# Attention of a hybrid decoder trunk: each group's tiles head by head, GpSimd's sums of weights issued after the values, VectorE's beside them, and two small steps of the row maxima on other engines

## The chip, the cores and the metric

The kernel runs on one core of a Trainium2 chip. The metric is the device time of one execution in microseconds (us). The core's engines are TensorE (PE in the profile; PEld is its loading of weights), VectorE (DVE), ScalarE (ACT), GpSimd (POOL) and SyncE (SP, which issues the DMAs). Each engine works through its own queue in order.

## The reference: what is computed

One decoder layer over 4096 positions of width 1024. An RMSNorm, one input projection, three token mixers side by side (a gMLP, a gated linear recurrence, and a forgetting attention), a gate for each, one output projection and a final RMSNorm. The change lies in the attention, 8 heads of 64:

```python
c = jnp.cumsum(jnp.transpose(log_f, (0, 2, 1)), axis=-1)
for blk in range(seq // C_BLOCK):
    ...
    s = jnp.einsum('bhqd,bhkd->bhqk', qh[:, :, q0:q1], kh[:, :, :q1]) * scale
    s = s + c[:, :, q0:q1, None] - c[:, :, None, :q1]
    s = jnp.where(mask[None, None], s, -jnp.inf)
    p = jax.nn.softmax(s, axis=-1)
    outs.append(jnp.einsum('bhqk,bhkd->bhqd', p, vh[:, :, :q1]))
```

## The kernel before

The program has three stages: the projection with the two other mixers (to about 1676 us), the attention (to about 3120 us), and the output projection.

The attention goes over 32 units. A unit is a pair of heads `p` (0 to 3) and a block `Q` of 512 queries (0 to 7). It has `4 * (Q + 1)` blocks of 128 keys; four of them are a group, so a unit has Q + 1 groups and there are 144 groups. The last group of a unit lies on the diagonal: its tiles are 512, 384, 256 and 128 queries wide, and each needs a mask.

For each key block and head one tile (n counts a group's eight tiles, 0 to 7) is made like this: two matmuls write the scores, keys by queries, into PSUM (`st`, lines 1374 and 1377, three buffers); ScalarE takes the exponential into `pt` (line 1381, 13 buffers); on the diagonal GpSimd masks a 128x128 piece of `pt` (line 1386). The tiles of a group are made in the order block 0 head 0, block 0 head 1, block 1 head 0, and so on. The products with the values (`pv`, line 1274, 16 matmuls for a group, two of them side by side in the array) come one group later: between the scores of tiles 2 and 3 of the following group.

The softmax divides by the sum of the weights over the keys. Each head has an SBUF tile `acc` of 128x512 into which the `pt` tiles are added (line 1261, or 1259 for the first two of a unit, 1257 for a copy): VectorE does it for head 0, GpSimd for head 1. A matmul with ones then sums `acc` over partitions (`pl`, line 1223). `finish_unit` follows: ScalarE copies `pv` out (1217) and makes 1/`pl` by Ln and Exp (1227, 1228), VectorE refines it (1230, 1231), GpSimd multiplies (1232, 1233, 1235), and a DMA stores `d_yc` (1236).

The row maxima for the softmax are computed ahead, by products of their own. `rowmax` makes two 128x512 tiles of scores at a time (`sm`, line 127, two buffers of two banks each), and VectorE reduces them from PSUM (line 140, or 135 on the diagonal). A group of the main loop takes four such steps (after tiles 0, 1, 4 and 6); more only while their count lags. When a unit's maxima are there, `rm_tail` makes its row: a maximum over the columns (159), the addition of `cref` (163), the negated copy `m2` (169), its rest in lower precision (170), some steps of the generator later a transposition on TensorE (`mt`, line 1181, which uses one of the two `sm` buffers) and a copy `mr` (1183).

TensorE's order is the order of the code. On the other engines a scheduler sets the order by its own estimate of when things are ready:

```python
ctx.enter_context(tc.manual_schedule(engines={mybir.EngineType.PE}))
```

Of the kernel before, what the change touches and what calls it, by code (L numbers as in the profile page):

```python
# [10 lines left out]
F32 = mybir.dt.float32  # L11
# [4 lines left out]
AF = mybir.ActivationFunctionType  # L16
ALU = mybir.AluOpType
# [4 lines left out]
P = 128  # L22
# [11 lines left out]
def tile_trunk(  # L34
# [16 lines left out]
    nc = tc.nc  # L51
    _, S, D = x.shape
    KC = D // P
    NSB = S // 256
    NJ = S // 512
# [22 lines left out]
    U0 = min(3, 2 * (NB - 1))  # L78
# [77 lines left out]
    def rm_rows(p, Q, mp, mm, m2):  # L156

        if Q > 0:
            nc.vector.tensor_reduce(mm, mp[:, :, : Q + 1], axis=AX.X, op=ALU.max)
            src = mm  # L160
        else:
            src = mp[:, :, 0]
        nc.vector.tensor_tensor(
            mm.rearrange("p (h i) -> p h i", h=2),
            src.rearrange("p (h i) -> p h i", h=2),
            bcast(cref[:, Q, 2 * p : 2 * p + 2][:, :, None], [P, 2, 4]),
            op=ALU.add,
        )
        nc.vector.tensor_scalar(m2[:, 0:8], mm, -1.0, None, op0=ALU.mult)
        nc.vector.scalar_tensor_tensor(  # L170
            m2[:, 8:16], mm, -1.0, m2[:, 0:8].bitcast(F32), op0=ALU.mult, op1=ALU.subtract
        )
# [919 lines left out]
    with ExitStack() as p2:  # L1092
        fs = p2.enter_context(tc.tile_pool(name="fs", bufs=3))
        ac = p2.enter_context(tc.tile_pool(name="ac", bufs=2))
# [18 lines left out]
        units = [(p, Q) for p in range(4) for Q in range(NJ)]  # L1113
        NU = len(units)
# [58 lines left out]
        def rm_tail(u, mp):  # L1173
            p, Q = units[u]
            mm = fs.tile([P, 8], F32, tag="mm", name="mm")
            m2 = fs.tile([P, 16], F32R, tag="m2", name="m2")
            rm_rows(p, Q, mp, mm, m2)
            for _ in range(2 if u == 0 else 3):
                yield
            pt = ps_sm.tile([16, P], F32, tag="sm", name="mt")  # L1180
            nc.tensor.transpose(pt, m2.bitcast(F32), ident)
            mr = fs.tile([16, P], F32R, tag="mr", name="mr", bufs=8)
            nc.vector.tensor_copy(mr, pt)
            mrow[u] = mr

        def unit_load(u):

            load_qa(u)
            qc = qc_t[u % 2]
            mr = d_m[u] if u < U0 else mrow.pop(u).bitcast(F32)  # L1190
            for r in range(2):
                nc.sync.dma_start(
                    qc[66 + r : 67 + r, :, :].rearrange("o h (i c) -> o (h i) c", c=P).bitcast(F32),
                    mr[8 * r : 8 * r + 8, :],
                )
# [42 lines left out]
        def q0_of(u, kb):  # L1238
            p, Q = units[u]
            j = kb - 4 * Q  # L1240
            return max(j, 0) * P, j >= 0

        fin = []

        first_pt = {}

        def do_acc(u, kb, h, pt):

            p, Q = units[u]
            q0, _ = q0_of(u, kb)  # L1250
            if kb == 0:
                if u not in acc_of:
                    acc_of[u] = [ac.tile([P, 512], F32, tag=f"acc{i}", name=f"acc{i}") for i in range(2)]
                first_pt[h] = pt
            eng, a = (nc.vector, nc.gpsimd)[h], acc_of[u][h]
            if Q == 0 and kb == 0:
                eng.tensor_copy(a, pt)
            elif Q and kb == 1:
                eng.tensor_tensor(a, first_pt[h], pt, op=ALU.add)
            elif kb:  # L1260
                eng.tensor_tensor(a[:, q0:], a[:, q0:], pt[:, q0:], op=ALU.add)  # L1261

        def do_pv(u, j, group):

            p, Q = units[u]
            nkb = 4 * (Q + 1)
            if j == 0:
                pv_of[u] = ps_pv.tile([P, 512], F32, tag="pv", name="pv")
            pv = pv_of[u]
            vt = v_t[p * NJ + j]  # L1270
            for kb, pts in group:
                q0, _ = q0_of(u, kb)
                for h in (1, 0):
                    nc.tensor.matmul(  # L1274
                        pv[64 * h : 64 * h + 64, q0:], vt[:, kb % 4, 64 * h : 64 * h + 64], pts[h][:, q0:],
                        start=kb == 0, stop=kb == nkb - 1,
                    )

            for kb, pts in group:
                do_acc(u, kb, 0, pts[0])  # L1280
            if j == Q:
                fin.append(finish_unit(u))
                tick(fin)
            if Q == NJ - 1:
                slots[0] += 2
                vslots[0] += 1
# [5 lines left out]
        def load_wo():  # L1292
            k = len(wo_hi)
            raw = big.tile([P, D], F32, tag="big", name="wor")
            hi = big.tile([P, D], F32R, tag="big", name="woh")
            lo = big.tile([P, D], F32R, tag="big", name="wol")
            nc.sync.dma_start(raw, wv[:, k, :])
            nc.scalar.copy(hi, raw)
            nc.vector.tensor_tensor(lo, raw, hi.bitcast(F32), op=ALU.subtract)
            wo_hi.append(hi)  # L1300
            wo_lo.append(lo)
# [16 lines left out]
        def load_next():  # L1318
            _, kind, i = need.popleft()
            slots[0] -= 1  # L1320
            if kind:
                vslots[0] -= 1
                load_ka(i)
            else:
                load_kb(i)

        def can_load():
            return slots[0] > 0 and (need[0][1] == 0 or vslots[0] > 0)
# [4 lines left out]
        def rm_step():  # L1333
            if not rm_live[0]:
                return

            while need and rm_next_kb() not in kb_t:
                assert can_load()
                load_next()
            try:  # L1340
                next(rm)
                rm_count[0] += 2
            except StopIteration:
                rm_live[0] = False
# [21 lines left out]
        def do_tile(u, kb, h):  # L1366

            p, Q = units[u]
            g = p * NJ + kb // 4
            cs = slice((kb % 4) * P, (kb % 4) * P + P)  # L1370
            q0, diag = q0_of(u, kb)
            qm = min(q0, 256)
            st = ps_st.tile([P, 512], F32, tag="st", name="st")
            nc.tensor.matmul(  # L1374
                st[:, qm:], ka_t[g][:, h, cs], qa_t[u % 2][:, h, qm:], start=True, stop=False
            )
            nc.tensor.matmul(  # L1377
                st[:, qm:], kb_t[g][0:68, h, cs], qc_t[u % 2][:, h, qm:], start=False, stop=True
            )
            pt = pp.tile([P, 512], F32, tag="p", name="pt")  # L1380
            nc.scalar.activation(  # L1381
                pt[:, q0:], st[:, q0:], AF.Exp, bias=bias_of[u][:, h, kb : kb + 1]
            )
            if diag:

                nc.gpsimd.affine_select(  # L1386
                    pt[:, q0 : q0 + P], pt[:, q0 : q0 + P], pattern=[[1, P]], compare_op=ALU.is_ge,
                    fill=0.0, base=0, channel_multiplier=-1,
                )
            return pt  # L1390

        pend, group = None, []
        for si, (u, kb) in enumerate(steps):
            p, Q = units[u]
            nkb = 4 * (Q + 1)
            while p * NJ + kb // 4 not in ka_t:
                load_next()
            if need and can_load() and need[0][0] < si + 48:
                load_next()
            elif not need and not rm_live[0] and len(wo_hi) < KC and slots[0] >= 3 and si % 2:  # L1400
                load_wo()
                slots[0] -= 2
            pts = []
            for h in range(2):
                pts.append(do_tile(u, kb, h))
                n = 2 * (kb % 4) + h
                if h == 1:
                    do_acc(u, kb, 1, pts[1])
                if n in (0, 1, 4, 6):
                    rm_step()  # L1410
                if n in (3, 5, 7) and rm_count[0] < 2 * si + LEAD:
                    rm_step()


                if n == 2 and pend is not None:
                    do_pv(*pend)
                    pend = None
                if n in (4, 5, 7):
                    tick(fin)
            group.append((kb, pts))  # L1420
            if kb % 4 == 3:
                pend, group = (u, kb // 4, group), []
            if kb == max(0, nkb - 4) and u + 1 < NU:
                while u + 1 >= U0 and u + 1 not in mrow:
                    rm_step()
                unit_load(u + 1)
                unit_bias(u + 1)
        do_pv(*pend)
        drain(fin)
        while len(wo_hi) < KC:  # L1430
# [106 lines left out]
```

## Time and profile before

| | before |
|---|---|
| median of 3 runs | 3488.28 us |
| lowest to highest | 3479.05 to 3490.75 us |
| profiled execution | 3480.39 us, span 3478.6 us |
| mean granted TensorE clock | 0.973 |
| PE, DVE, ACT, POOL busy | 96%, 69%, 46%, 42% of the span |
| attention, 1676 to 3120 us | 1444 us of the span |

The span is the time from the first to the last instruction of the profiled execution. A line number such as L1261 is the line of the kernel before. A busy PE is modelled: a half-speed clock shows in the column PEclk and not as idle time, so both have to be read.

### The profile page before, as it was taken

Reading aid. Unit: us, or ns where it says so; the run is one execution under the profiler, and the core shown is the slowest. Engines: PE = TensorE matmul, PEld = TensorE weight load, DVE = VectorE, ACT = ScalarE, POOL = GpSimd, SP = SyncE. Lnnn points to the kernel's source line nnn. Section 1 sums busy time; section 2 is a strip of 40 time slices with the busy share of each in tenths; the row PEclk is TensorE's granted clock in tenths of the full one; section 3 lists DMA queues with packets and bytes.
Section 4 is the critical chain, followed back from the end, with each engine's and each line's share of the span. In section 5 each row is a group of like instructions: output and inputs, shape, how many; then the busy total and the mean of one; then the engine's idle time right before and its main releaser. Section 6 shows DMA issues by size and latency. Waiting matters only on the chain.

```text
span 3478.6 us, 62964 instructions
## 1 busy us (share of the span) xinstructions
PE 3324.5 (96%) x24375; PEld 2627.7 (76%) x24375; DVE 2385.7 (69%) x4615; ACT 1607.1 (46%) x2915; POOL 1458.1 (42%) x1472
## 2 busy tenths in 40 slices
PE   7999999999999999999799899999999999999998
PEld 7999999999999999989455455555555555548887
DVE  6467746586467755684588878777877888765554
ACT  6335553456344553353255455555545555552221
POOL 2134422343233421253366567666766676670000
PEclk9999999999999999999799999999999999999999
DMA  5332243215232133212641141014201311023442
GB/s 180 111 95 65 83 137 116 78 53 165 86 104 80 51 97 115 80 38 67 143 113 31 50 117 49 19 46 120 59 22 31 103 56 43 22 70 139 146 145 97
DMA packets 227598, 297.71 MB, mean 86 GB/s; under 512 B 19602, under 2 KB 172448, under 8 KB 227298
## 3 DMA queue, kind: packets, MB, share of 16 engines
q1 hardware_dynamic: 227298, 293.69, 28.0%
q8 instruction: 191, 3.13, 0.4%
q14 instruction: 109, 0.89, 0.1%
HBM read 208.96 MB, written 84.43 MB: 84 GB/s over the span
## 4 chain that ended last, share of the span: by engine, by line
PE 71%; DVE 19%; ACT 4%; issue 3%; DMA 2%; POOL 2%; SPq 0%; DVEq 0%; ACTq 0%; POOLq 0%
PE acc L902 16%; PE pv L1274 13%; PE acc L923 12%; PE o L1475 10%; PE sm L127 6%; PE st L1374 6%; PE st L1377 5%; DVE mp L140 4%; DVE acc L1261 3%; DVE wlo L228 2%; DMA x<-in_x_dram 1%; PE pl L1223 1%; DVE gt L746 1%; DVE xq L511 1%; PE xtp L284 1%
## 5 line engine op out<-in xcount | busy, mean ns | idle before, releaser
L1381 ACT ACTIVATE pt<-st,bias 128x512 f32<-128x512 f32 (+3 forms) x1152 | 698.7, 651 | 630.2 <-PE st L1377 582.3
L1261 POOL TENSOR_TENSOR acc<-acc,pt 128x512 f32<-128x512 f32 (+2 forms) x516 | 672.4, 1303 | 329.8 <-ACT pt L1381 302.0
L140 DVE TENSOR_REDUCE mp<-sm 128x2 f32<-128x1024 f32 (+1 forms) x460 | 534.8, 1192 | 223.5 <-PE sm L127 222.7
L902 PE MATMUL acc<-hhi,whi 128*128 128x256 f32 x2048 | 581.0, 288 | 3.1 <-DVE s L760 1.9
L902 PE MATMUL acc<-hhi,wlo 128*128 128x256 f32 x2048 | 568.5, 282 | 0.0
L902 PE MATMUL acc<-hlo,whi 128*128 128x256 f32 x2048 | 567.9, 282 | 0.0
L923 PE MATMUL acc<-whi,hhi 128*128 128x256 f32 (+1 forms) x1792 | 518.7, 289 | 18.1 <-DVE gu L744 16.0
L1274 PE MATMUL pv<-pt,v 128*64 128x512 f32 (+3 forms) x2304 | 510.1, 587 | 0.0
L923 PE MATMUL acc<-wlo,hhi 128*128 128x256 f32 (+1 forms) x1792 | 507.7, 283 | 0.0
L923 PE MATMUL acc<-whi,hlo 128*128 128x256 f32 (+1 forms) x1792 | 507.3, 283 | 0.0
L1261 DVE TENSOR_TENSOR acc<-acc,pt 128x512 f32<-128x512 f32 (+2 forms) x516 | 458.8, 889 | 43.1 <-POOL pt L1386 17.1
L1374 PE MATMUL st<-qa,ka 128*128 128x512 f32 (+2 forms) x1152 | 468.4, 409 | 19.6 <-DMA v<-d_v 13.2
L1377 PE MATMUL st<-qc,kb 68*128 68x512 f32 (+2 forms) x1152 | 444.2, 387 | 0.0
L127 PE MATMUL sm<-kb,qb 66*128 66x512 f32 (+2 forms) x1152 | 367.0, 400 | 61.1 <-DVE mp L140 36.4
L902 PEld LDWEIGHTS acc<-hhi,whi 128*128 128x128 f32 x2048 | 385.6, 190 | 6.6 <-issue 1.9
L902 PEld LDWEIGHTS acc<-hlo,whi 128*128 128x128 f32 x2048 | 384.8, 190 | 0.3 <-DVE hlo L290 0.2
L902 PEld LDWEIGHTS acc<-hhi,wlo 128*128 128x128 f32 x2048 | 384.6, 190 | 0.0
L1274 PEld LDWEIGHTS pv<-pt,v 128*64 128x64 f32 x2304 | 159.0, 143 | 297.6 <-issue 279.7
L1374 PEld LDWEIGHTS st<-qa,ka 128*128 128x128 f32 x1152 | 221.1, 192 | 191.4 <-issue 133.1
L923 PEld LDWEIGHTS acc<-whi,hhi 128*128 128x128 f32 x1792 | 342.2, 191 | 21.9 <-DVE gu L744 16.6
L923 PEld LDWEIGHTS acc<-wlo,hhi 128*128 128x128 f32 x1792 | 342.8, 191 | 0.1
L923 PEld LDWEIGHTS acc<-whi,hlo 128*128 128x128 f32 x1792 | 342.2, 191 | 0.0
(265 smaller groups left out, 5113.9 us busy)
## 6 DMA issues: line engine op xcount, KB each, us to landing
wraw<-in_w_in_dram SPq DMA_DIRECT2D x120, 512.0 KB
x<-in_x_dram SPq DMA_DIRECT2D x88, 512.0 KB
qa<-d_qh SPq DMA_DIRECT2D x64, 256.0 KB
out_dram<-x SPq DMA_DIRECT2D x31, 512.0 KB
kb<-d_kh SPq DMA_DIRECT2D x38, 256.0 KB
d_kh<-chi SPq DMA_DIRECT2D x32, 256.0 KB
d_kl<-clo SPq DMA_DIRECT2D x32, 256.0 KB
d_qh<-chi SPq DMA_DIRECT2D x32, 256.0 KB
```

The costliest lines, as they stand in the source:

```text
L127: nc.tensor.matmul(ps[:, :n], qb[0:66, h, i * P : (i + 1) * P], kb[0:66, h, :n], start=True, stop=True)
L140: nc.vector.tensor_reduce(dst, ps, axis=AX.X, op=ALU.max)
L228: nc.vector.scalar_tensor_tensor(lo[:, k, :n], raw, g, hi[:, k, :n].bitcast(F32), op0=ALU.mult, op1=ALU.subtract)
L284: nc.tensor.transpose(pt[:, k, :], xts[half][:, c * P : (c + 1) * P], ident)
L902: nc.tensor.matmul(ps[:, a, :], ww[:, k, cs], hh[:, k, :], start=n == 0, stop=n == 3 * KC - 1)
L923: nc.tensor.matmul(o, hh[:, k, ts_], ww[:, k, :width], start=n == 0, stop=n == 3 * KC - 1)
L1261: eng.tensor_tensor(a[:, q0:], a[:, q0:], pt[:, q0:], op=ALU.add)
L1274: nc.tensor.matmul(pv[64 * h : 64 * h + 64, q0:], vt[:, kb % 4, 64 * h : 64 * h + 64], pts[h][:, q0:], start=kb == 0, stop=kb == nkb - 1,)
L1374: nc.tensor.matmul(st[:, qm:], ka_t[g][:, h, cs], qa_t[u % 2][:, h, qm:], start=True, stop=False)
L1377: nc.tensor.matmul(st[:, qm:], kb_t[g][0:68, h, cs], qc_t[u % 2][:, h, qm:], start=False, stop=True)
L1381: nc.scalar.activation(pt[:, q0:], st[:, q0:], AF.Exp, bias=bias_of[u][:, h, kb : kb + 1])
L1475: nc.tensor.matmul(ps, a[:, k % 4, o : o + P], b[k][:, cs], start=n == 0, stop=n == 3 * KC - 1)
```

## The change

It does five things.

1. The main loop runs over groups, and a group's eight tiles are made head by head: blocks 0 to 3 of head 1 first (n 0 to 3), then those of head 0 (n 4 to 7).
2. GpSimd's four sums (head 1) of a group are issued together after tile 3 of the same group, and the first of them waits, by an added dependency, for that tile's first score matmul. TensorE makes this matmul just after the values of the group before.
3. VectorE's four sums (head 0) are issued together with the values of their group, and the first of them waits for the first matmul of these values.
4. In `rm_rows` the addition of `cref` goes from VectorE to GpSimd, and the negated copy from VectorE to ScalarE.
5. The transposition in `rm_tail` comes six steps of the generator later instead of three, and the loads and the bias of the next unit are issued after tile 2 of a unit's last group and not after tile 1.

```diff
@@ rm_rows
-        nc.vector.tensor_tensor(
+        nc.gpsimd.tensor_tensor(
             mm.rearrange("p (h i) -> p h i", h=2),
...
-        nc.vector.tensor_scalar(m2[:, 0:8], mm, -1.0, None, op0=ALU.mult)
+        nc.scalar.activation(m2[:, 0:8], mm, AF.Copy, scale=-1.0)
@@ rm_tail
-            for _ in range(2 if u == 0 else 3):
+            for _ in range(2 if u == 0 else 6):
@@
-        def do_acc(u, kb, h, pt):
+        def behind(inst, other):
+            tc.add_manual_dep(
+                inst.ins, other.ins.name, mybir.DependencyInfo(mybir.DependencyClass.Sync, mybir.DependencyReason.DATA),
+                reason="sums wait for their turn",
+            )
+
+        def do_accs(u, j, pts, h, other):
...
+            if j == 0 and Q == 0:
+                behind(eng.tensor_copy(a, pts[0]), other)
+            for i in range(1 if j == 0 else 0, 4):
+                q0, _ = q0_of(u, 4 * j + i)
+                src = pts[0] if j == 0 and Q and i == 1 else a
+                ins = eng.tensor_tensor(a[:, q0:], src[:, q0:], pts[i][:, q0:], op=ALU.add)
+                if i == 1 - (j > 0) and not (j == 0 and Q == 0):
+                    behind(ins, other)
@@ do_pv
-            for kb, pts in group:
-                do_acc(u, kb, 0, pts[0])
+            do_accs(u, j, group[0], 0, first)
@@ main loop
-        for si, (u, kb) in enumerate(steps):
+        for gi, (u, j) in enumerate((u, j) for u, (p, Q) in enumerate(units) for j in range(Q + 1)):
...
+            for n in range(8):
+                h, i, si = 1 - n // 4, n % 4, 4 * gi + n // 2
...
+                pt, first = do_tile(u, 4 * j + i, h)
+                group[h].append(pt)
+                if n == 3:
+                    do_accs(u, j, group[1], 1, first)
...
+                if n == 2 and j == Q and u + 1 < NU:
+                    while u + 1 >= U0 and u + 1 not in mrow:
+                        rm_step()
+                    unit_load(u + 1)
+                    unit_bias(u + 1)
```

The changed kernel's lines stand a few further down: 1261 is 1263 there (with 1259 for a copy), 1274 is 1280, 1374 and 1377 are 1380 and 1383, 1381 is 1387, 1386 is 1392.

The order on VectorE where a unit's maxima end (unit Q = 1 of the second head pair, the stretch from 2344 us on in the trace of before). Before:

```order
L140 TENSOR_REDUCE mp<-sm 128x2 [waits PE_49]
L1261 TENSOR_TENSOR acc_27274<-acc_27274,pt 128x512 [waits Activation_49]
L159 TENSOR_REDUCE mm<-mp 128x8 [waits DVE_49]
L1261 TENSOR_TENSOR acc_27274<-acc_27274,pt 128x512 [waits DVE_49,Activation_49]
L163 TENSOR_TENSOR mm<-mm,cref 128x8 [waits DVE_49]
L1261 TENSOR_TENSOR acc_27274<-acc_27274,pt 128x512 [waits DVE_49,Activation_49]
L169 TENSOR_SCALAR m_27413<-mm 128x8 [waits DVE_49]
L170 SCALAR_TENSOR_TENSOR m_27413<-mm,m_27413 128x8 [waits DVE_49]
L140 TENSOR_REDUCE mp<-sm 128x2 [waits PE_49]
```

The same unit's maxima in the changed kernel, where `PE_49` on a sum is the added wait for the values:

```order
L1263 TENSOR_TENSOR acc_26739<-acc_26739,pt 128x512 [waits PE_49,Pool_49]
L135 ISA sm,mp<-sm,tri 128x512 [waits DVE_49]
L135 ISA mp 128x1
L1263 TENSOR_TENSOR acc_26739<-acc_26739,pt 128x384 [waits DVE_49,Pool_49]
L159 TENSOR_REDUCE mm<-mp 128x8 [waits DVE_49]
L1263 TENSOR_TENSOR acc_26739<-acc_26739,pt 128x256 [waits DVE_49,Pool_49]
L170 SCALAR_TENSOR_TENSOR m_27362<-mm,m_27362 128x8 [waits Activation_49]
L1263 TENSOR_TENSOR acc_26739<-acc_26739,pt 128x128 [waits DVE_49]
L140 TENSOR_REDUCE mp<-sm 128x2 [waits PE_49] x2
```

Two small steps (163, 169) have left VectorE's queue, and line 170 waits for ScalarE now; the sums stand in one block behind the start of the values, with the maxima of that stretch ahead of them or behind.

The order on GpSimd at the end of a unit (unit Q = 4 of the third head pair). Before:

```order
L1386 AFFINE_SELECT pt<-pt 128x128 [waits Activation_49] x2
L1261 TENSOR_TENSOR acc_28507<-acc_28507,pt 128x512 [waits Pool_49]
L1386 AFFINE_SELECT pt<-pt 128x128 [waits Activation_49] x2
L1261 TENSOR_TENSOR acc_28507<-acc_28507,pt 128x384 [waits Pool_49]
L1386 AFFINE_SELECT pt<-pt 128x128 [waits Activation_49] x2
L1261 TENSOR_TENSOR acc_28507<-acc_28507,pt 128x256 [waits Pool_49]
L1386 AFFINE_SELECT pt<-pt 128x128 [waits Activation_49] x2
L1203 TENSOR_TENSOR bias<-cref,ctok 128x2x24
L1261 TENSOR_TENSOR acc_28507<-acc_28507,pt 128x128 [waits Pool_49]
```

In the changed kernel:

```order
L1392 AFFINE_SELECT pt<-pt 128x128 [waits Activation_49] x3
L1263 TENSOR_TENSOR acc_28553<-acc_28553,pt 128x512 [waits PE_49,Pool_49]
L1392 AFFINE_SELECT pt<-pt 128x128 [waits Activation_49]
L1263 TENSOR_TENSOR acc_28553<-acc_28553,pt 128x384 [waits Pool_49]
L1263 TENSOR_TENSOR acc_28553<-acc_28553,pt 128x256 [waits Pool_49]
L1392 AFFINE_SELECT pt<-pt 128x128 [waits Activation_49]
L1263 TENSOR_TENSOR acc_28553<-acc_28553,pt 128x128 [waits Pool_49]
L1392 AFFINE_SELECT pt<-pt 128x128 [waits Activation_49] x3
L1203 TENSOR_TENSOR bias<-cref,ctok 128x2x24
L163 TENSOR_TENSOR mm<-mm,cref 128x8 [waits DVE_49]
```

The masks of head 0 (the last four) now stand behind the four sums of head 1, the first of which waits for TensorE, and line 163 is the last thing before the next block of sums.

More of the change, by code (lines that the diff above doesn't have):

```diff
@@ L1243, in tile_trunk @@
         fin = []
-        first_pt = {}
-        def do_acc(u, kb, h, pt):
-            p, Q = units[u]
[L1250 to L1254, printed above, removed]
-            eng, a = (nc.vector, nc.gpsimd)[h], acc_of[u][h]
[L1256 to L1261, printed above, removed]
+        def behind(inst, other):
[4 more added lines that the diff above has]
+        def do_accs(u, j, pts, h, other):
+            p, Q = units[u]
+            if u not in acc_of:
+                acc_of[u] = [ac.tile([P, 512], F32, tag=f"acc{i}", name=f"acc{i}") for i in range(2)]
+            eng, a = (nc.vector, nc.gpsimd)[h], acc_of[u][h]
+            if j == 0 and Q == 0:
[6 more added lines that the diff above has]
+                    behind(ins, other)
         def do_pv(u, j, group):
@@ L1270, in do_pv @@
             vt = v_t[p * NJ + j]
-            for kb, pts in group:
+            first = None
+            for i in range(4):
+                kb = 4 * j + i
                 q0, _ = q0_of(u, kb)
                 for h in (1, 0):
-                    nc.tensor.matmul(
-                        pv[64 * h : 64 * h + 64, q0:], vt[:, kb % 4, 64 * h : 64 * h + 64], pts[h][:, q0:],
+                    mm = nc.tensor.matmul(
+                        pv[64 * h : 64 * h + 64, q0:], vt[:, i, 64 * h : 64 * h + 64], group[h][i][:, q0:],
                         start=kb == 0, stop=kb == nkb - 1,
                     )
-            for kb, pts in group:
-                do_acc(u, kb, 0, pts[0])
+                    first = first or mm
+            do_accs(u, j, group[0], 0, first)
             if j == Q:
@@ L1373, in do_tile @@
             st = ps_st.tile([P, 512], F32, tag="st", name="st")
-            nc.tensor.matmul(
+            first = nc.tensor.matmul(
                 st[:, qm:], ka_t[g][:, h, cs], qa_t[u % 2][:, h, qm:], start=True, stop=False
@@ L1389, in do_tile @@
                 )
-            return pt
-        pend, group = None, []
-        for si, (u, kb) in enumerate(steps):
+            return pt, first
+        pend = None
+        for gi, (u, j) in enumerate((u, j) for u, (p, Q) in enumerate(units) for j in range(Q + 1)):
             p, Q = units[u]
[L1395 to L1408, printed above, removed]
+            group = [[], []]
+            for n in range(8):
+                h, i, si = 1 - n // 4, n % 4, 4 * gi + n // 2
+                if n % 2 == 0:
+                    while p * NJ + j not in ka_t:
+                        load_next()
+                    if need and can_load() and need[0][0] < si + 48:
+                        load_next()
+                    elif not need and not rm_live[0] and len(wo_hi) < KC and slots[0] >= 3 and si % 2:
+                        load_wo()
+                        slots[0] -= 2
+                pt, first = do_tile(u, 4 * j + i, h)
+                group[h].append(pt)
+                if n == 3:
+                    do_accs(u, j, group[1], 1, first)
                 if n in (0, 1, 4, 6):
@@ L1419, in tile_trunk @@
                     tick(fin)
[L1420 to L1427, printed above, removed]
+                if n == 2 and j == Q and u + 1 < NU:
[3 more added lines that the diff above has]
+                    unit_bias(u + 1)
+            pend = (u, j, group)
         do_pv(*pend)
```

## The prediction

> **What bounds the kernel now.** I read the page's busy shares first, then the busy time by stretches, then who TensorE waited for, and last the order of time at one of its waits. All terms come from the attention between 1750 and 3090 us; the projection and the output product are in the same order before and after, but for the small row-maximum steps. Busy time by stretches (columns: PE, PEld, DVE, ACT, POOL, granted clock, DMA share, GB/s):
>
> ```profile
> 2536.00:2587.00 51.00, 50.89 (x228) 29.50 (x225) 39.79 (x47) 27.85 (x46) 32.76 (x32) 1.00 0.09 26
> 2349.00:2352.00 3.00, 0.79 (x3) 0.44 (x2) 2.96 (x5) 1.19 (x2) 2.41 (x2) 0.94 1.08 255
> 2352.00:2358.00 6.00, 5.38 (x13) 2.45 (x14) 5.36 (x8) 1.37 (x2) 1.78 (x1) 0.50 0.41 90
> 1750.00:3090.00 1340.00, 1282.72 (x5548) 721.37 (x5545) 1082.08 (x1571) 715.86 (x1185) 878.80 (x865) 0.97 0.21 58
> ```
>
> In the middle of a unit (first row) TensorE is busy for 50.89 of 51.00 us at full clock: nothing that moves work between the other engines can win there. At the start of some units (second and third row) TensorE stands, and then runs at half clock for about six microseconds. Over the whole stretch it is idle for 1340.00 - 1282.72 = 57.3 us, and a mean clock of 0.97 costs some 40 us more (33 to 47, as the figure is rounded). So about 97 us are there to be won, and no more. Who TensorE waited for, same stretch (total, times, longest):
>
> ```profile
> PE sm L127 <- DVE mp L140: 33.7, 29, 2.2
> PE sm L127 <- DVE mp L135: 15.6, 25, 3.0
> PE mt L1181 <- DVE mp L140: 1.8, 5, 0.6
> ```
>
> Of the 57.3 us, 33.7 + 15.6 = 49.3 are row-maximum products that wait for an `sm` buffer, which VectorE frees late. Why late, in order of time, VectorE first, then GpSimd, then TensorE:
>
> ```profile
> 2344.07 1.47 DVE L1261 TENSOR_TENSOR acc<-acc,pt 128x512 f32<-128x512 f32 x1
> 2345.46 0.16 DVE L159 TENSOR_REDUCE mm<-mp 128x8 f32<-128x16 f32 x1
> 2345.64 1.59 DVE L1261 TENSOR_TENSOR acc<-acc,pt 128x512 f32<-128x512 f32 x1
> 2347.15 1.25 DVE L163 TENSOR_TENSOR mm<-mm,cref 128x8 f32<-128x8 f32 x1
> 2348.33 0.68 DVE L1261 TENSOR_TENSOR acc<-acc,pt 128x512 f32<-128x512 f32 x1
> 2348.93 1.24 DVE L169 TENSOR_SCALAR m<-mm 128x8 fp32r<-128x8 f32 x1
> 2350.20 0.17 DVE L170 SCALAR_TENSOR_TENSOR m<-mm,m 128x8 fp32r<-128x8 f32 x1
> 2350.28 1.22 DVE L140 TENSOR_REDUCE mp<-sm 128x2 f32<-128x1024 f32 x1
> ...
> 2343.71 1.28 POOL L1261 TENSOR_TENSOR acc<-acc,pt 128x512 f32<-128x512 f32 x1
> 2344.95 1.73 POOL L1235 TENSOR_TENSOR rt<-rt,rc 128x512 f32<-128x512 f32 x1
> 2347.01 4.48 POOL L1261 TENSOR_TENSOR acc<-acc,pt 128x512 f32<-128x512 f32 x3 [0.33 <-ACT pt L1381]
> ...
> 2348.25 0.40 PE L1374 MATMUL st<-qa,ka 128*128 128x512 f32 x1
> 2348.49 0.40 PE L1377 MATMUL st<-qc,kb 68*128 68x512 f32 x1
> 2351.56 1.17 PE L127 MATMUL sm<-kb,qb 66*128 66x512 f32 x2 [2.21 <-DVE mp L140]
> 2354.42 1.22 PE L127 MATMUL sm<-kb,qb 66*128 66x512 f32 x2 [0.62 <-DVE mp L140]
> ```
>
> Between two reductions VectorE spends 2344.07 to 2350.28, 6.2 us, on three sums and the row's small steps. One sum takes 0.68 us here and another 1.59, and additions over 8 elements take as long as one of GpSimd's sums (4.48 us for 3): while GpSimd works on a tile from SBUF, a VectorE step that adds two SBUF tiles makes no progress. TensorE then waits 2.21 us. Waits of 2.2 us like this one stand at six places; the first and the last:
>
> ```profile
> 1992.56 0.73 PE L127 MATMUL sm<-kb,qb 66*128 66x512 f32 x2 [2.21 <-DVE mp L140]
> 2889.86 0.73 PE L127 MATMUL sm<-kb,qb 66*128 66x512 f32 x2 [2.21 <-DVE mp L140]
> ```
>
> **The change, part by part.** Prices from the groups by shape between 1750 and 3090 us (count, busy us, mean ns), and the shortest, median and longest of the two small steps:
>
> ```profile
> L1261 DVE TENSOR_TENSOR acc<-acc,pt 128x512 f32<-128x512 f32 x404 | 394.5, 976 | 21.8 <-ACT pt L1381 6.1 <-POOL pt L1386 2.7 <-DVE acc L1261 0.5
> L1261 POOL TENSOR_TENSOR acc<-acc,pt 128x512 f32<-128x512 f32 x403 | 577.1, 1432 | 309.5 <-ACT pt L1381 287.9
> L140 DVE TENSOR_REDUCE mp<-sm 128x2 f32<-128x1024 f32 x408 | 485.7, 1219 | 179.4 <-PE sm L127 179.0
> L163 DVE TENSOR_TENSOR mm<-mm,cref x25: 151/164/1255, 1758.3 to 3032.7; 128x8 f32<-128x8 f32 x25
> L169 DVE TENSOR_SCALAR m<-mm x28: 156/172/1235, 1759.6 to 3032.9; 128x8 fp32r<-128x8 f32 x28
> L1203 POOL TENSOR_TENSOR bias<-cref,ctok x28: 198/248/291, 1757.9 to 2982.3; 128x40 f32<-128x40 f32 x4, 128x48 f32<-128x48 f32 x4, 128x56 f32<-128x56 f32 x4, 128x64 f32<-128x64 f32 x4
> L1386 POOL TENSOR_SCALAR_AFFINE_SELECT pt<-pt 128x128 f32<-128x128 f32 x231 | 75.5, 340 | 61.3 <-ACT pt L1381 61.3
> L1233 POOL TENSOR_TENSOR rc<-rc,rn 128x512 f32<-128x512 f32 x29 | 46.6, 1608 | 4.5 <-DVE rn L1231 4.5
> L1261 POOL TENSOR_TENSOR acc<-acc,pt 128x384 f32<-128x384 f32 x29 | 29.2, 1006 | 2.4
> L1261 POOL TENSOR_TENSOR acc<-acc,pt 128x256 f32<-128x256 f32 x29 | 21.6, 744 | 2.4
> L1261 POOL TENSOR_TENSOR acc<-acc,pt 128x128 f32<-128x128 f32 x29 | 13.4, 461 | 0.1
> L1381 ACT ACTIVATE pt<-st,bias 128x128 f32<-128x128 f32 x58 | 20.8, 364 | 5.9 <-PE st L1377 5.7
> ```
>
> *Sums placed apart.* No sum is added or removed. VectorE's four of a group now start with the values, GpSimd's four after them. A group's values take 3.65 us (row below) and VectorE's four sums 4 x 0.68 = 2.7 us, if GpSimd is silent. GpSimd's four take 5.1 us at the 1.28 us of the first GpSimd row above, and between one group's values and the next TensorE has about 5.6 us (eight score tiles and four maximum products of two matmuls each, 0.235 us from one start to the next as in the two score rows above). They fit, with 0.5 us over. The added wait holds up on VectorE only the maxima behind the sums; those products come at the earliest two score tiles and a product after the values, so 1.4 us of slack cover it. With 4 x 1.22 + 2.7 = 7.6 us of about 9.3 a group, VectorE keeps up. So most late buffers go: of the 49.3 us I leave 11 in place, because the product right after a transposition has only one free buffer (the 0.62 us row; about 25 unit ends at some 0.45), and take 85% of the other 38: **32 us**.
>
> *Small steps moved.* 25 times L163 and 28 times L169 leave VectorE. On GpSimd the nearest row is the bias (0.25 us), on ScalarE the shortest exponential (0.36 us); neither engine bounds. L170 now waits for both. Its place is inside the values, where GpSimd is done with its sums and ScalarE has no scores. Bounds: nothing, or at the seven unit starts where ScalarE's copy of `pv` stands behind L169, some 0.7 us, since the `pl` product waits for that copy: 5 us lost.
>
> *The clock.* The six places of 2.2 us carry about 6 us at 0.50 each: 6 x 3 = 18 us, and smaller clusters of waits carry the rest of the 40. If the waits go, so does this: I take **30 us** (18 to 40).
>
> *Transposition six steps later, loads and bias one tile later.* The first takes away the 1.8 us of line 1181 and some lateness of `mr`; but where a unit's row is needed before its lead suffices (the last unit of the first head pair), the loop forces four extra maxima at once: 2 to 4 us, once or twice. The loads stand in SP's queue, not TensorE's; SP waits there for buffers that scores free, not for its place in the code, so they cost nothing; GpSimd's bias is needed by the next unit's first exponential, five tiles later. Net -2 us.
>
> *Start of the attention* (1676 to 1750 us): the same effect on 74 us that run mostly at low clock: 5 us, bounds 0 to 10.
>
> Sum: 32 + 30 + 5 - 5 - 2 = 60 us off the profiled execution's 3480.39 us: **3420 us**. That execution is 7.9 us below the median of 3488.28 and inside the runs shown; 0.3%, some 10 us, is about what a measurement of this kernel can tell from no change.
>
> *GpSimd's queue at a unit's end.* Behind the waiting sum stand the masks of head 0 and the bias, and the next values wait for the last of these masks. From the start of values to the next:
>
> ```profile
> 2501.59 3.65 PE L1274 MATMUL pv<-pt,v 128*64 128x512 f32 x16
> 2509.84 2.37 PE L1274 MATMUL pv<-pt,v 128*64 128x512 f32 x16
> ```
>
> From 2505.24 to 2509.84 are 4.6 us; by my estimate from the 0.235 us of a 512-wide score matmul the tiles left after tile 3 are 0.35 us longer in the new order, the fourth pair of values comes 1.0 us after the first, and tile 3 itself takes 0.24: 5.7 us. GpSimd needs 1.43 + 1.01 + 0.74 + 0.46 + 5 x 0.34 = 5.3 us. It just fits, so I cost it at nothing, but the cover is thin.
>
> **The rivals.** (a) *GpSimd's masks come late* and the values wait at all 32 unit ends: this is the slower side. What speaks for it is the 0.4 us of margin at mean prices; against it, the 1.28 us of an undisturbed sum, which leaves half a microsecond. Below a lateness of 1 us it takes back 32 us at most; from 1.9 us on (60 / 32) it outweighs the gain, and at 2.2 us with a half clock behind it, as in the rows above, each end costs 2.2 + 3.0: 32 x 5.2 = 166, so 3586 us.
>
> (b) *The finishing products collide.* L1233 and L1235, about 1.6 us each, follow GpSimd's third sum in a unit's first group and run into the next values, against VectorE's sums: 3.2 us late less 1.4 to 2 of slack, some 1 us at 28 ends: 3448 us. The Trainium skill, SBUF — State Buffer, "SBUF: two separate sides", says that VectorE and GpSimd share one pair of ports by an exclusive lock held for a whole instruction; the trace agrees (1.25 us for 8 elements). By that rule in full, without the slack, 28 x 3.2 = 90 us would eat the whole gain.
>
> (c) *The half clock stays* although single waits go, through many waits of 0.5 us: 3420 + 30 = 3450 us. The Trainium skill, TensorE: Matmul & The Clock Gate, "What's actually happening", has the clock fall after an idle window of about 3.4 us; here a wait of 2.21 us was followed by 0.50, so the trace is stricter than a whole idle window.
>
> (d) *VectorE's load, not the place of its sums, makes the maxima late* (it is busy 1082 of 1340 us); then only the two small steps help, 2.5 us at six places: 3465 us.
>
> (e) *It does not do what it says where it matters*: the middle of a unit has no waits, and new waits at the ends replace the old: 3470 to 3498 us.
>
> **How the numbers follow.** My case 0.56 (3390 to 3440: 90 us is nearly all that is lost, 40 is the waits at half effect), (b) 0.12, (c) 0.08, (d) 0.06; these are all faster by over 0.3%: 0.82. (e), within 0.3%: 0.08. (a), slower: 0.10. The range reaches from 3390 over (b), (c) and (d) to 3470, which leaves out (a) and (e).
>
> **What would show it.** Right: TensorE's idle time between 1750 and 3090 us falls from 57 to some 25 us, no wait of 2.2 us on line 127 is left, the clock rises to 0.99, a VectorE sum falls from 976 towards 700 ns and GpSimd's from 1432 towards 1300. Wrong: TensorE's values waiting for GpSimd's masks, `pl` waiting for ScalarE, or line 127 still waiting with sums at 976 ns.

## The result, and the profile after

The changed kernel takes 3448.99 us (median; 3443.33 to 3452.37), against 3489.52 for the kernel before on the same chip: a ratio of 0.9894, 95% interval 0.9877 to 0.9912. Run again later beside other kernels it took 3451.44 us, ratio 0.9911 (0.9897 to 0.9926). So it is faster by 31 to 41 us; 60 were forecast off the profiled execution, 68 off the median. The two profiled executions (3480.39 and 3452.37 us) differ by 28 us, since the one before lies low and the one after high among their runs. From the first score matmul to the first output product, the attention takes 1417.3 us where it took 1446.7: 29 us shorter, which is the whole difference between the two executions.

Busy time by stretches of the changed kernel, for the stretch of the prediction (columns as there):

```profile
1750.00:3090.00 1340.00, 1298.96 (x5617) 741.68 (x5615) 1081.36 (x1527) 736.62 (x1236) 865.74 (x910) 0.98 0.21 59
```

Idle time of TensorE went from 57.3 to 1340.00 - 1298.96 = 41.0 us, and the clock from 0.97 to 0.98, not 0.99. Who TensorE waited for, same stretch:

```profile
PE sm L127 <- DVE mp L140: 24.4, 27, 2.1
PE st L1380 <- ACT pt L1387: 5.5, 4, 3.4
PE pl L1223 <- DVE acc L1263: 4.2, 4, 1.2
PE sm L127 <- DVE mp L135: 2.1, 4, 1.3
PE pl L1223 <- ACT rt L1217: 1.7, 5, 0.3
```

Line 127 now waits 26.5 us where it waited 49.3. New is line 1223, `pl`, waiting for VectorE. 4.9 of the 5.5 us of line 1380 stand behind 3050 us, at the end of the attention; before, 5.5 us like them stand behind 3090. The groups by shape, after:

```profile
L1263 DVE TENSOR_TENSOR acc<-acc,pt 128x512 f32<-128x512 f32 x413 | 348.1, 843 | 81.2 <-PE pv L1280 50.1 <-POOL pt L1392 1.4 <-DVE acc L1263 0.5
L1263 POOL TENSOR_TENSOR acc<-acc,pt 128x512 f32<-128x512 f32 x411 | 554.9, 1350 | 294.9 <-PE st L1380 217.6 <-PE st L1383 52.3 <-ACT m L169 2.9
L1263 DVE TENSOR_TENSOR acc<-acc,pt 128x128 f32<-128x128 f32 x30 | 25.0, 832 | 2.4
L1223 PE MATMUL pl<-acc,ones_v 128*64 128x512 f32 x116 | 48.2, 618 | 5.8 <-DVE acc L1263 4.2 <-ACT rt L1217 1.7
L163 POOL TENSOR_TENSOR mm<-mm,cref 128x8 f32<-128x8 f32 x25 | 13.5, 542 | 52.9 <-DVE mm L159 46.8 <-PE st L1383 6.2
```

and before, the two rows that answer to its third and fourth:

```profile
L1223 PE MATMUL pl<-acc,ones_v 128*64 128x512 f32 x116 | 31.3, 618 | 0.0
L1261 DVE TENSOR_TENSOR acc<-acc,pt 128x128 f32<-128x128 f32 x29 | 8.5, 295 | 0.9 <-POOL pt L1386 0.9
```

VectorE's 512-wide sum fell from 976 to 843 ns, GpSimd's from 1432 to 1350. But VectorE's last sum of a unit, 128 wide, went from 295 to 832 ns, and the row sums that need it keep TensorE busy for 48.2 us where it was 31.3. In order of time at one unit's end, after (VectorE, GpSimd, TensorE):

```profile
2151.90 0.42 DVE L1263 TENSOR_TENSOR acc<-acc,pt 128x256 f32<-128x256 f32 x1
2152.66 0.98 DVE L170 SCALAR_TENSOR_TENSOR m<-mm,m 128x8 fp32r<-128x8 f32 x1 [0.34 <-ACT m L169]
2153.56 0.28 DVE L1263 TENSOR_TENSOR acc<-acc,pt 128x128 f32<-128x128 f32 x1
...
2152.35 1.26 POOL L1263 TENSOR_TENSOR acc<-pt 128x512 f32<-128x512 f32 x1
2153.58 1.39 POOL L1232 TENSOR_TENSOR rt<-rt,zt 128x512 f32<-128x512 f32 x1
...
2153.15 1.81 PE L1223 MATMUL pl<-acc,ones_v 128*64 128x512 f32 x4 [0.34 <-ACT rt L1217]
...
2167.64 0.27 PE L1181 MATMUL mt<-ident,m 128*16 128x128 f32 x1
2168.75 0.73 PE L127 MATMUL sm<-kb,qb 66*128 66x512 f32 x2 [0.83 <-DVE mp L140]
```

and a `pl` of the kernel before:

```profile
2418.26 1.08 PE L1223 MATMUL pl<-acc,ones_v 128*64 128x512 f32 x4
```

L170 waits for the copy that moved to ScalarE, then takes 0.98 us beside a GpSimd sum; the unit's last sum starts late and ends only at 2153.84. (At 17 of the 30 unit ends it is that last sum itself that takes 1.17 to 1.24 us, beside GpSimd's additions and products.) Head 1's row sum has begun by then, head 0's follows it instead of running beside it: 1.81 us, not 1.08, and nothing of that shows as idle. The last two rows are a loss that the change left: a product right behind the transposition waits, since one `sm` buffer is the transposition's and the other still holds maxima. Going through the waits in order of time, line 127 waits 20.9 us at 23 such places after, and 21.8 us at 26 before; at all other places it fell from 30.4 to 6.3 us (sums of all its waits, those for other releasers too).

### The profile page after: what moved, and what is told of

Read it like the earlier page. It is cut to its first block, busy times and chain, and to the rows that moved or that the text cites. A ratio compares the mean times of both kernels' runs of the same rounds, so it can differ in the third digit from the quotient of the medians.

```text
span 3450.7 us, 62925 instructions
## 1 busy us (share of the span) xinstructions
PE 3316.0 (96%) x24375; PEld 2634.7 (76%) x24375; DVE 2367.5 (69%) x4551; ACT 1614.1 (47%) x2947; POOL 1428.7 (41%) x1504
## 4 chain that ended last, share of the span: by engine, by line
PE 72%; DVE 18%; ACT 3%; DMA 2%; POOL 2%; issue 2%; SPq 0%; DVEq 0%; POOLq 0%; ACTq 0%
PE acc L902 16%; PE pv L1280 12%; PE acc L923 11%; PE o L1481 10%; PE st L1380 7%; PE sm L127 6%; PE st L1383 6%; DVE mp L140 3%; DVE acc L1263 3%; DVE wlo L228 2%; DMA x<-in_x_dram 2%; PE pl L1223 1%; DVE gt L746 1%; DVE xq L511 1%; PE plb L574 1%
## 5 line engine op out<-in xcount | busy, mean ns | idle before, releaser
L1263 POOL TENSOR_TENSOR acc<-acc,pt 128x512 f32<-128x512 f32 (+2 forms) x516 | 639.0, 1238 | 303.1 <-PE st L1380 221.3
L1263 DVE TENSOR_TENSOR acc<-acc,pt 128x512 f32<-128x512 f32 (+2 forms) x516 | 414.4, 803 | 91.7 <-PE pv L1280 51.7
L127 PE MATMUL sm<-kb,qb 66*128 66x512 f32 (+2 forms) x1152 | 359.2, 394 | 33.2 <-DVE mp L140 26.0
L923 PEld LDWEIGHTS acc<-whi,hhi 128*128 128x128 f32 x1792 | 341.8, 191 | 22.3 <-DVE gu L744 16.6
```

What stands on the lines that cost most here:

```text
L127: nc.tensor.matmul(ps[:, :n], qb[0:66, h, i * P : (i + 1) * P], kb[0:66, h, :n], start=True, stop=True)
L923: nc.tensor.matmul(o, hh[:, k, ts_], ww[:, k, :width], start=n == 0, stop=n == 3 * KC - 1)
L1263: ins = eng.tensor_tensor(a[:, q0:], src[:, q0:], pts[i][:, q0:], op=ALU.add)
```

## The experiments

My theory (A): the gain comes from sums that stand apart; a new wait takes part of it back, that of `pl` for VectorE's last sums, and an old one keeps another part, that of the product behind the transposition. (When I wrote the expectations I took this second one for grown.) Rival (B): the gain is VectorE's, freed of two small steps. Waits and groups below are of the stretch 1750 to 3050 us, where VectorE's 512-wide sum takes 953 ns in the kernel before and 841 in the changed one; the waits of line 127 are the same there as above (33.7 and 15.6; 24.4 and 2.1).

**The small steps alone.** On the kernel before:

```diff
-        nc.vector.tensor_tensor(mm..., cref..., op=ALU.add)      # line 163
+        nc.gpsimd.tensor_tensor(mm..., cref..., op=ALU.add)
-        nc.vector.tensor_scalar(m2[:, 0:8], mm, -1.0, None, op0=ALU.mult)
+        nc.scalar.activation(m2[:, 0:8], mm, AF.Copy, scale=-1.0)
```

> The kernel before, with only the two small steps of the row maxima moved (line 163 to GpSimd, line 169 to ScalarE); tiles, sums and the transposition's place stay. Theory A (the gain comes from the sums, which stand apart, so that VectorE's are short and the maxima are not late): little of the 40 us comes, 3470 to 3490 us, VectorE's 512-wide sum stays near 976 ns and most of the 2.2 us waits on line 127 stay. Theory B (the gain is VectorE's, freed of the two small steps): most of it comes, 3450 to 3460 us, and the 2.2 us waits go.

3465.67 us, ratio 0.9948 (0.9934 to 0.9961): 18 us, between the two theories. VectorE's sum stays at 956 ns, as A had it, but no wait of 2.2 us is left, as B had it. Its waits:

```profile
PE sm L127 <- DVE mp L140: 21.6, 23, 2.0
PE sm L127 <- DVE mp L135: 14.1, 25, 1.4
```

**All but the small steps.** The changed kernel with these two lines as before.

> The changed kernel with the two small steps back on VectorE; all else as changed. Theory A: the gain stays nearly whole, 3448 to 3462 us, VectorE's sum near 845 ns. Theory B: the gain goes, 3475 to 3490 us, with the 2.2 us waits on line 127 back.

3450.79 us, ratio 0.9905 (0.9893 to 0.9918): the same as the changed kernel. Its sum and its waits:

```profile
L1263 DVE TENSOR_TENSOR acc<-acc,pt 128x512 f32<-128x512 f32 x398 | 324.3, 815 | 67.1 <-PE pv L1280 36.3 <-DVE acc L1263 0.9 <-issue 0.5
```

```profile
PE sm L127 <- DVE mp L140: 24.5, 28, 1.9
PE pl L1223 <- DVE acc L1263: 6.7, 7, 1.1
```

The new order, with its added waits and the later transposition, brings the whole gain without the steps. The steps help by 18 us where maxima are late anyway and by nothing where they are not: two ways to remove the same waits, which do not add. Rival B falls as the cause of this change's gain.

**What GpSimd's additions cost.** This kernel leaves out GpSimd's sums but the first of each unit, and takes both heads' row sums from VectorE's, so its output is not the attention's; only its time is of use. On the kernel before:

```diff
-            elif kb:
+            elif kb and h == 0:
                 eng.tensor_tensor(a[:, q0:], a[:, q0:], pt[:, q0:], op=ALU.add)
...
-                nc.tensor.matmul(pl[...], ones_v, acc[h], start=True, stop=True)
+                nc.tensor.matmul(pl[...], ones_v, acc[0], start=True, stop=True)
```

> The kernel before without GpSimd's weight sums beyond the first tile of a unit, about 400 additions; the row sums of both heads are taken from VectorE's (the output is that of other sums, the order of the rest is kept). It measures what GpSimd's additions cost VectorE. If VectorE's sums are slow because GpSimd adds at the same time, its 512-wide sum falls from 976 ns to 690 to 750, the 2.2 us waits on line 127 go, and the time falls by 30 to 60 us, to 3430 to 3460. If VectorE's own load makes the maxima late (the rival), the sum stays above 900 ns and the time moves by less than 15 us.

3406.67 us, ratio 0.9781 (0.9767 to 0.9794): 77 us, more than I had expected.

```profile
L1261 DVE TENSOR_TENSOR acc<-acc,pt 128x512 f32<-128x512 f32 x412 | 326.2, 792 | 43.8 <-ACT pt L1381 30.3 <-POOL pt L1386 1.2 <-DVE acc L1261 0.5
```

```profile
PE sm L127 <- DVE mp L140: 20.7, 23, 2.0
PE sm L127 <- DVE mp L135: 2.8, 8, 1.1
```

The mean is above the 750 expected, since 26 first-tile additions and GpSimd's finishing products stay: laid over GpSimd's records, 325 of the 412 sums have no GpSimd instruction beside them and take 668 to 695 ns; the slow ones stand beside those left. So VectorE's sums are slow through GpSimd, and the kernel before loses 77 us through the additions. What is left of line 127's waits is the loss behind the transposition: 22.3 us at 26 places by the count above, so GpSimd's additions don't make it.

**The two added waits.** The changed kernel without both, then with VectorE's alone, then with GpSimd's alone (`behind` not called for the other):

```diff
-                behind(eng.tensor_copy(a, pts[0]), other)
+                eng.tensor_copy(a, pts[0])
...
-                if i == 1 - (j > 0) and not (j == 0 and Q == 0):
-                    behind(ins, other)
```

> The changed kernel without the two added waits: the sums keep their new places in the order, but start as soon as their engine and their tiles are ready. Theory A in its strong form (the waits keep VectorE's and GpSimd's additions apart): the sums meet again, VectorE's 512-wide sum goes from 843 ns towards 976, and the time goes up 5 to 25 us, to 3455 to 3475. Theory A in its weak form (the place in the order does it, and the wait only makes the row sums of lines 1223 late): no more than 5 us slower, or up to 15 us faster, since VectorE's last sums end earlier and the second row-sum matmul waits less. Theory B: no change.

> The changed kernel with VectorE's added wait alone; GpSimd's sums are free to start, and to stand in GpSimd's order, as early as their tiles. Without both waits it took 3542. If VectorE's wait does the work (sums behind the maxima on VectorE), the time stays below 3465. If GpSimd's wait does it (masks ahead of sums, and additions apart), it is 3500 or more. If each does a part, 3465 to 3500.

> The changed kernel with GpSimd's added wait alone; VectorE's sums are free. If GpSimd's wait does the work, the time stays below 3465, or falls under the 3449 of both waits by up to 15, since VectorE's last sums of a unit end earlier and the row sums wait less. If VectorE's wait does it (its sums otherwise stand ahead of the maxima's reductions), it is 3500 or more. If each does a part, 3465 to 3500.

Without both 3542.27 us, ratio 1.0171 (1.0158 to 1.0184); with VectorE's alone 3516.59, 1.0084 (1.0068 to 1.0099); with GpSimd's alone 3565.30, 1.0230 (1.0211 to 1.0249). All are slower than the kernel before. The first is far outside what I had set; the other two both fall in the case of 3500 or more, so in this order of tiles each wait is needed. Waits without both:

```profile
PE sm L127 <- DVE mp L140: 40.4, 52, 3.7
PE sm L127 <- DVE mp L135: 22.1, 25, 1.4
PE pl L1223 <- DVE acc L1263: 16.5, 14, 3.2
```

With VectorE's wait alone, its sums and the waits:

```profile
L1265 DVE TENSOR_TENSOR acc<-acc,pt 128x512 f32<-128x512 f32 x373 | 385.4, 1033 | 61.7 <-PE pv L1282 33.7 <-issue 1.7 <-DVE acc L1265 0.5
```

```profile
PE sm L127 <- DVE mp L140: 26.3, 27, 2.7
PE pl L1223 <- DVE acc L1265: 20.1, 16, 1.6
```

With GpSimd's wait alone, its sums, the waits, and the stretch:

```profile
L1265 DVE TENSOR_TENSOR acc<-acc,pt 128x512 f32<-128x512 f32 x356 | 302.5, 850 | 24.5 <-POOL pt L1394 12.7
```

```profile
PE sm L127 <- DVE mp L135: 46.6, 25, 3.1
PE sm L127 <- DVE mp L140: 39.7, 54, 3.9
```

```profile
1750.00:3050.00 1300.00, 1195.49 (x5016) 673.03 (x5015) 938.62 (x1409) 646.59 (x1087) 764.57 (x814) 0.95 0.21 55
```

One of its waits in order of time (VectorE, then TensorE):

```profile
2186.76 0.94 DVE L1265 TENSOR_TENSOR acc<-acc,pt 128x512 f32<-128x512 f32 x1 [2.02 <-POOL pt L1394]
2187.63 0.55 DVE L135 CUSTOM_DVE_ANT_0 sm<-sm,tri 128x384 f32<-128x384 f32 x1
...
2189.49 0.68 PE L127 MATMUL sm<-kb,qb 66*128 66x384 f32 x2 [3.14 <-DVE mp L135]
```

The two waits do different things, and neither does it alone. GpSimd's keeps the additions apart: without it VectorE's sum is 1033 ns, and `pl` waits 20 us for it. VectorE's keeps the sums behind the maxima: without it the scheduler puts sums ahead of reductions in VectorE's order. Here VectorE stands 2.02 us before a sum whose mask isn't there, with the reductions queued behind it, and TensorE waits 3.14 us. The sums themselves are quick (850 ns), yet line 127 waits 86 us and the clock falls to 0.95. Taking a wait out changes the scheduler's order as well as the time of a start; which of the two weighs more was not tried. Head by head without the waits is worse than tile by tile; why, these runs don't isolate.

**Row sums one tile later** (on the changed kernel):

```diff
-                if n in (4, 5, 7):
+                if n in (5, 6, 7):
                     tick(fin)
```

> The changed kernel with the row sums of a finished unit (line 1223) one tile later, behind the sixth tile of the next step in place of the fifth. Theory A2 (the changed kernel pays about 0.7 us per unit since head 0's row-sum matmul waits for VectorE's last sums and the two heads no longer run together): the pair in line 1223 goes from 1.8 us back to about 1.1, and the time falls by 10 to 22 us, to 3427 to 3439. Rival (the pair's length is not waited for, since it only shifts work that the clock or ScalarE bounds): within 5 us of 3449.

**Transposition behind the values**, held until tile 4:

```diff
             for _ in range(2 if u == 0 else 6):
                 yield
+            while tile_n[0] != 4:
+                yield
...
+                tile_n[0] = n                 # in the main loop, at each tile
```

> The changed kernel with the transposition of the row maxima held until the fifth tile of a step, so that it stands behind the values and not right behind a product of line 127. Theory A3 (the product behind the transposition waits about 1 us, at 25 unit ends, because one of the two PSUM buffers is the transposition's and the other still holds maxima): those waits of 1.8 to 2.4 us go, and the time falls by 12 to 25 us, to 3424 to 3437. Rival (the maxima are then late at the next unit's masks, or the wait moves to the next product): within 5 us, or slower by up to 10.

**Both.**

> The changed kernel with both: the row sums one tile later and the transposition behind the values. Theories A2 and A3 together: the two losses add, 22 to 45 us below the changed kernel, 3404 to 3427. Rivals: no more than the better of the two alone.

The run of the changed kernel beside them:

> The changed kernel once more, on the chip of these runs, for the comparison: 3443 to 3453 us, about 40 below the kernel before.

| kernel | median, us | ratio to before, interval | attention, us |
|---|---|---|---|
| changed kernel | 3451.44 | 0.9911, 0.9897 to 0.9926 | 1420.2 |
| row sums later | 3435.02 | 0.9865, 0.9850 to 0.9880 | 1403.3 |
| transposition later | 3439.84 | 0.9883, 0.9863 to 0.9902 | 1407.5 |
| both | 3427.43 | 0.9843, 0.9828 to 0.9858 | 1395.4 |

16, 12 and 24 us below the changed kernel in the same comparison: the first within what I had set (10 to 22), the second just under it (12 to 25), the two together near the lower end (22 to 45). The middle one's intervals overlap with the changed kernel's, the others' do not. Row sums later:

```profile
L1223 PE MATMUL pl<-acc,ones_v 128*64 128x512 f32 x116 | 38.6, 618 | 1.5 <-DVE acc L1263 1.5
```

That is 9.6 us less busy and 4.3 us less waiting, 14 of the 16 us. Transposition later (its lines 1226 and 1266 are 1223 and 1263 of the changed kernel):

```profile
PE pl L1226 <- DVE acc L1266: 11.9, 7, 2.6
PE sm L127 <- DVE mp L140: 4.1, 7, 1.4
PE st L1386 <- DMA qc<-mr: 2.2, 2, 1.6
PE sm L127 <- DVE mp L135: 2.0, 6, 0.9
```

The 26.5 us of line 127 fall to 6.1, but 7.7 come back at `pl`: where one wait goes, the row sums are late next. So both losses were real, one that the change made and one that it left, and together they are worth some 24 us. "Both" is the fastest of the four.

**VectorE's last sum, freed of GpSimd.** On "both", first GpSimd's sums of a unit's first group one tile later, then also the finishing product that needs no row sums behind the row-sum matmuls:

```diff
-                if n == 3:
+                if n == (3 if j else 4):
                     do_accs(u, j, group[1], 1, first)
```

```diff
-            nc.gpsimd.tensor_tensor(t, t, zt, op=ALU.mult)
+            behind(nc.gpsimd.tensor_tensor(t, t, zt, op=ALU.mult), last)    # last: matmul of pl
```

> The kernel with both repairs (row sums one tile later, transposition behind the values), and GpSimd's sums in the first step of a unit begin one tile later, behind the fifth tile's score product. Theory (VectorE's last, 128-wide sum of the unit before takes 1044 ns in place of 290 since GpSimd adds or multiplies beside it, and so head 0's row-sum matmul is late): that sum falls to 300 to 500 ns, the 9.5 us of waits of line 1226 for VectorE fall under 4, and the time falls by 5 to 15 us below the 3427 of the kernel with both repairs, to 3412 to 3422. Rival (the collision only moves, to the sums of the next step or to GpSimd's finishing products, or the masks behind GpSimd's sums come late): within 4 us of 3427, or slower by up to 15.

> The kernel of the run before last (both repairs, GpSimd's sums in a unit's first step one tile later), and GpSimd's product of a finished unit that needs no row sums (rt by zt, line 1232 of the changed kernel) waits for the row-sum matmuls. There, at 2446.5 us, that product starts beside VectorE's last sum of a unit, which then takes 1392 ns in place of 290. Theory (VectorE stands still until GpSimd's instruction ends): the 128-wide sum falls from 1206 ns to 290 to 450, the waits of the row sums for VectorE from 9.8 us to under 3, and the time by 5 to 12 us, to 3416 to 3423. Rival (row sums that come late are by now covered by other work, or the later product collides with VectorE's next sums): within 4 us of 3428, or slower by up to 10, also where the 128-wide sum does fall.

3428.30 us, ratio 0.9833 (0.9816 to 0.9850), and 3434.49 us, 0.9859 (0.9835 to 0.9882): no gain on "both" in either, as the rivals had it. VectorE's 128-wide sum in "both", then in the second of them:

```profile
L1266 DVE TENSOR_TENSOR acc<-acc,pt 128x128 f32<-128x128 f32 x29 | 30.3, 1044 | 2.4
```

```profile
L1266 DVE TENSOR_TENSOR acc<-acc,pt 128x128 f32<-128x128 f32 x29 | 18.0, 622 | 2.4
```

```profile
PE pl L1226 <- DVE acc L1266: 8.8, 5, 2.2
```

The first edit only moved the collision (1206 ns, now beside `rt` by `zt`). The second halved the sum's time, and the row sums still wait 8.8 us, at five places of up to 2.2 us. So at the other units the 128-wide sum, slow or not, is no longer waited for once the row sums stand a tile later. What makes VectorE late at those five stays open.

## Why the prediction was right or wrong

The direction and the mechanism held: additions placed apart, quicker sums, fewer late maxima. 3449 lies in the range, in its upper half, but the gain is 31 to 41 us where 60 were added up: TensorE's idle time fell to 41 us and not to 25, VectorE's sum to 843 ns and not towards 700. The terms:

- *Waits for late maxima, 32 us:* 22.8 came (49.3 to 26.5). The failed step is the 11 us left in place behind the transposition, 25 unit ends at some 0.45 us: by the count above it was 26 at 0.84, 21.8 us, and it stayed. I had taken one row, of 0.62 us, for the rest. The other factor held: at the other places 24 of 30.4 us went, 79% where I took 85. And I booked the six-step delay as a small gain without asking which tile it would stand at: in both kernels it follows tile 1, with a product on each side: the one of tile 0, whose maxima still hold a buffer, and the one of tile 1, which waits.
- *Clock, 30 us:* 0.97 to 0.98, so 13 us by the rounded figures, which leave anything up to 27 open. The whole spans, with a digit more (3478.6 us at 0.973, 3450.7 at 0.979), lose 93.9 and 72.5 us to it: 21 us, the start of the attention included. The six 2.2 us waits went, but 23 behind the transposition, most of them 0.74 to 0.86 us and one of 2.1, stayed, which is rival (c) in part.
- *Small steps, -5 us:* the loss that I named (`pl` behind ScalarE) is 1.7 us. The one that counts was not in the sum: `pl` waits for VectorE's last sums, which the change lets start only with the values of their group. That is 16.9 us of longer matmuls (48.2 - 31.3) and 4.2 of waits; 16 came back with one tile more. I had asked what stands behind the waiting sum on VectorE, found the maxima, and overlooked that TensorE's `pl` is a reader of that sum. The steps' own gain was nothing in the new order, as the run without them shows.
- *Start of the attention, 5 us:* the values of the sixth group begin at 1755.6 us where they began at 1758.3, though the attention began 1.6 us later: some 4 us, near the forecast, in this execution; in a second profile of the changed kernel it is 1.8. *Transposition and forced steps, -2:* line 1181 itself waits 0.2 us where it waited 2.5; the forced steps are not separated.

The whole account, from the stretches of the attention before and after:

```profile
1674.00:3121.00 1447.00, 1375.33 (x5869) 772.57 (x5869) 1152.55 (x1664) 760.08 (x1258) 930.52 (x928) 0.96 0.24 64
1676.00:3093.00 1417.00, 1369.18 (x5868) 782.40 (x5869) 1133.90 (x1606) 766.61 (x1287) 898.87 (x957) 0.97 0.24 65
```

TensorE's idle time fell from 71.7 to 47.8 us, 24 us, the new waits of `pl` already taken off. Its busy time fell by 6 us although the row sums take 17 more, so the rest of its work takes 23 us less, which is about the clock's 21. 24 + 23 - 17 = 30 us. Against the sum of 60, waits and clock came some 8 us short each, and the 17 us of the row sums were not in it.

Of the rivals, (a) did not come: TensorE's matmuls wait 0.6 us for a mask in the whole stretch, its loads of the values' weights 9.5 us, at 18 places. (b), at 3448 us, hit the time, by luck as far as the runs show: its collision is there (a sum of VectorE beside L1235 takes 1578 ns at 2162 us, the next, beside GpSimd's own sums, 1660), but it is not new. Between 1750 and 3090 us 67 of VectorE's 512-wide sums stood beside L1233 or L1235 in the kernel before, 1324 ns in the mean, and 50 in the changed one, 1247 ns. What it costs in time was not taken apart. (d) had 3465 for the small steps alone, and they gave 3465.67; but the sums' place gave more. (e) did not come. The Trainium skill, SBUF — State Buffer, "SBUF: two separate sides", has an exclusive lock that makes the other engine stand for a whole instruction; the 128-wide sums of 832 to 1206 ns, and 290 where GpSimd is silent, agree for GpSimd's additions and products.

## What to carry to other kernels

When a sum, a copy or a reduction is started later on purpose, list every reader of its result, not only what is queued behind it, and move the readers by as much: here the row sums, for 16 us. Two matmuls that run side by side lose their overlap when one operand is late, and that shows as longer busy time and not as a wait. When two edits remove the same wait, time each alone before adding their gains.

## What was not expected of the hardware

In the changed kernel VectorE's 512-wide addition has two speeds rather than a mean: of the 413 between 1750 and 3090 us, 337 take under 700 ns and 63 over 1400. Up to 3050 us, a unit's first sums included, 269 of 423 have no GpSimd instruction beside them and take 675 to 694 ns, while the 70 beside GpSimd's sums alone take 683 to 1819 (mean 1196). There, who starts first goes on: where the sum starts before GpSimd's addition or product it takes 679 to 695 ns (50 sums), where it starts after, 1574 in the median (72). In the kernel before, the order of the starts does not part them so clearly (668 to 1796 ns where GpSimd starts first). So the prediction's reading, that VectorE makes no progress while GpSimd works on a tile, is too wide. GpSimd's masks take part in this, and mostly it is the mask that stands: in the kernel before, 23 masks start inside a sum of VectorE, take 611 to 762 ns where one with no such sum beside it takes 288 in the median, and end 150 to 153 ns behind that sum.

VectorE's reductions from PSUM are not touched: 1219 ns in both kernels. An 8-element step can cost 0.98 us on VectorE beside GpSimd's sums, and GpSimd's own 8-element addition (L163) takes 542 ns in the mean, where I had set 250 by the bias.
